# Latent attention's scores by row halves with stacked rotary parts, and each attention step's scores placed behind the values of the step before it

## The chip, the cores and the metric

The kernel runs on one core of one Trainium2 chip. The metric is the device time of one execution in microseconds (us); three runs of the kernel before gave 1801.73, 1802.9 and 1808.01 us, median 1802.9. The engines are TensorE (PE; its weight loads are a row of their own, PEld), VectorE (DVE), ScalarE (ACT), GpSimd (POOL) and SyncE (SP, which issues most DMAs).

## The reference

A two-layer backbone works on 512 latent tokens and 256 context tokens of width 1024. In each layer one input projection feeds four groups, whose outputs are concatenated and projected back; a squared-ReLU MLP follows. The groups are neighbourhood attention (A), banded window attention (B), latent attention (C) and a state-space scan (D). The change is mostly in C, cut here to what matters:

```
q  = (rmsnorm(cq)  @ w_uq ).reshape(B, L, 4, 64 + 32)    # 4 heads, 64 plain + 32 rotary features
kv = (rmsnorm(ckv) @ w_ukv).reshape(B, L, 4, 64 + 64)
qn, qr = q[..., :64], q[..., 64:];  kn, v = kv[..., :64], kv[..., 64:]
qr, kr = axial_rope(qr), axial_rope(kr)                  # latent tokens; kr is one for all heads
s = (einsum('bqhd,bkhd->bhqk', qn, kn) + einsum('bqhd,bkd->bhqk', qr, kr)) * 96 ** -0.5
p = softmax(s);  o = einsum('bhqk,bkhd->bqhd', p, v)
```

A latent query sees all 768 keys, a context query only the 256 of the context. In the second layer the context's outputs are not needed, so there are no context queries.

## The kernel before

Products are made in fp32r from split operands: x = hi + lo, and hi·hi, lo·hi and hi·lo are added up in PSUM. `dense` (L247 on, its matmuls on L261) makes 24 matmuls of 128 rows for each block of 128 outputs and each segment (512 latent or 256 context tokens). A weight block comes by DMA from SP, ACT casts the high part (L238) and DVE makes the low one (L239).

All three attentions go through `attend` (L390). One call is a *step*: 128 queries, two heads. It makes the scores in banks of the PSUM pool `ps_s` (4 banks of 512 columns, also used by the preparation of latent attention and by the scan), the row minimum on DVE (L441 with two key parts, L449 with one), the exponential on ACT (L455), reciprocal and scaling (L460, L462 on DVE with two parts, L464 on ACT with one), the transposes of the probabilities on TensorE (L473), their copies to SBUF (L374 ACT, L376 DVE) and the product with the values (L479). The last value matmul of each step is appended to the list `anchors`. Window and neighbourhood attention call it with `paired=True`: heads lie in rows 0 to 63 and 64 to 127, and their score matmuls alternate (L418), each placed behind the one before it. Latent attention's heads have 96 rows, its scores are made head by head (L431), and no score is tied to another step.

A step has 768 score columns per head in latent attention when its queries are latent (a *full* step; 4 banks for two heads), and 256 when they are context tokens (a *context* step). The first layer has 12 latent steps (two head pairs with 4 full steps and 2 context steps each), the second 8 full ones. They are called A1, A2 and so on here, and those of window attention B1, B2 and so on.

Instructions are put in order ahead of time by a list scheduler: on each engine the earliest instruction of the program that is ready by its simulated clock comes next. `tc.issue_after(x)` forbids an instruction to come before x on its engine. Other work is interleaved in program order by `merge(*(generator, weight))`, which always advances the generator with the smallest (count + 0.5) / weight. Beside latent attention (weight 12 in the first layer, 11 in the second) runs `calls` (weight 6 and 11): in the first layer the projections sq1 and sk, three rotary steps, and the projections nq0, nk0, nq1, nk1; in the second the same without sq1. Each goes through `behind` (LAG = 2), so that it comes after the values of the last step but one of those already in the program. Beside window attention's 12 and 8 steps run six convolution projections and two for gates (weights 11 and 12), beside neighbourhood attention's the scan and the first half of the output projection.

Before its steps the latent generator (`mla`) normalises, makes the queries (`queries`, L1031), rotates their rotary part, copies both parts into one 96-row tile per head (L1035, L1038, L1048), transposes the rotary key (L1056) and writes it into each head's key tile as hi and lo (L1020, L1021), and makes the plain keys (L1063) and values (L1069). The yields in it count for `merge`: queries, rotary keys, plain keys, values, then the steps.

The norm ahead of the MLP ends in `rest`, a generator: its first advance makes the sums and the reciprocal root on DVE, the second the broadcast on TensorE (L308), the others the modulated activations of the last token piece. The first NAHEAD blocks of the MLP (3 and 5) advance it.

Of the kernel before, what the change touches and what calls it, by code (L numbers as in the profile page):

```python
# [72 lines left out]
QORD = (0, 1, 2)  # L73
# [18 lines left out]
def kernel(ctx: ExitStack, tc: tile.TileContext, D: dict, out: bass.AP, dbg=None):  # L92
# [157 lines left out]
    def dense(src, acts, segs, evac, ks=range(KD), w=None, low=V, midway=None):  # L250
# [139 lines left out]
    def attend(q, k, parts, sinks, vt, put, sgn=-1.0, paired=False):  # L390
# [14 lines left out]
        if paired:  # L405


            off, prev = 0, None
            for k0, n, tab in parts:
                if off == 0 or off + n - b0 > 512:  # L410
                    banks, b0 = (pss(), pss()), off
                dst = [banks[a][:, off - b0:off - b0 + n] for a in range(2)]
                nmm = len(terms(0))
                for i in range(nmm):
                    for a in range(2):
                        x, y = terms(a)[i]
                        with (tc.issue_after(prev.ins) if prev else nullcontext()):
                            prev = PE.matmul(dst[a], x, y[:, k0:k0 + n], start=i == 0, stop=i == nmm - 1)  # L418
                for a in range(2):
                    ats[a].append((dst[a], off, n, tab))  # L420
                off += n
        else:
            for a in range(2):
                off = 0
                for k0, n, tab in parts:
                    if off == 0 or off + n - b0 > 512:
                        bank, b0 = pss(), off
                    dst = bank[:, off - b0:off - b0 + n]
                    mm = terms(a)
                    for i, (x, y) in enumerate(mm):  # L430
                        PE.matmul(dst, x, y[:, k0:k0 + n], start=i == 0, stop=i == len(mm) - 1)  # L431
                    ats[a].append((dst, off, n, tab))
                    off += n
# [205 lines left out]
    for l in range(DEPTH):  # L639
# [329 lines left out]
        def mla():  # L969
# [36 lines left out]
            for b in range(4):  # L1006
# [4 lines left out]
            qh = [unit("u", nm("qh")) for _ in range(4)]  # L1011
            kh = [(unit("u", nm("kh"), F32R), unit("u", nm("kl"), F32R)) if SR[2] else unit("u", nm("kh"))
                  for _ in range(4)]

            def put_k(hd, r0, r1, c0, n, ps):
                if not SR[2]:
                    evac(kh[hd][r0:r1, c0:c0 + n], ps)
                    return
                hi, lo = (x[r0:r1, c0:c0 + n] for x in kh[hd])
                A.copy(hi, ps)  # L1020
                V.tensor_tensor(lo, ps, hi.bitcast(F32), ALU.subtract)  # L1021

            vm = [unit("u", nm("vm")) for _ in range(2)]

            def queries():
                msc = -(96.0 ** -0.5)
                for b in QORD:
                    for s, c0, n in segs:
# [4 lines left out]
                        if b < 2:  # L1033
                            for e in range(2):
                                A.activation(qh[2 * b + e][0:64, c0:c0 + n], ps[64 * e:64 * e + 64, :n], AF.Copy, scale=msc)  # L1035
                        elif s == 1:
                            for hd in range(4):
                                A.activation(qh[hd][64:96, c0:c0 + n], ps[32 * hd:32 * hd + 32, :n], AF.Copy, scale=msc)  # L1038
                        else:
                            qr, qs = unit("q", nm("qr")), unit("q", nm("qs"))  # L1040
                            A.activation(qr[:, :SEQ], ps, AF.Copy, scale=msc)
# [4 lines left out]
                            for hd in range(4):  # L1046
                                rs_ = slice(32 * hd, 32 * hd + 32)
                                V.tensor_tensor(qh[hd][64:96, 0:SEQ], qr[rs_, :SEQ], qs[rs_, :SEQ], ALU.add)  # L1048
# [4 lines left out]
            for s, c0, n in full:  # L1053
                pk = pss()
                for t in range(n // P):
                    PE.transpose(pk[0:32, t * P:(t + 1) * P], krr[:, c0 // P + t, :], ident)  # L1056
                for hd in range(4):
                    put_k(hd, 64, 96, c0, n, pk[0:32, 0:n])
            yield
            for b in range(2):  # L1060
                for s, c0, n in full:
                    ps = pss()
                    PE.matmul(ps[:, :n], wkv[:, b * P:(b + 1) * P], ckv[:, c0:c0 + n], start=True, stop=True)  # L1063
                    for e in range(2):
                        put_k(2 * b + e, 0, 64, c0, n, ps[64 * e:64 * e + 64, :n])
# [8 lines left out]
            for b in range(2):  # L1074
                om = unit("u", nm("om"))
                for j in range(WS // P):
# [7 lines left out]
                    qs = [qh[2 * b + a][0:96, cs] for a in range(2)]  # L1084
                    ks = [kh[2 * b + a] for a in range(2)]
                    if SR[2]:
                        qs = [tuple(x[0:96] for x in split_q(x, 96)) for x in qs]
# [381 lines left out]
```

## Time and profile before

| | |
|---|---|
| Profiled execution, its own time | 1802.71 us |
| its span, first to last instruction | 1800.9 us |
| PE busy | 1750.6 us (97%) |
| DVE busy | 1109.4 us (62%) |
| ACT busy | 737.8 us (41%) |
| POOL busy | 240.3 us (13%) |
| mean granted clock of TensorE | 0.987 |
| chain that ended last, PE's share | 89% |

Busy times are unions of an engine's instruction spans. Matmuls overlap in a pipeline, so the time that one costs is the distance from its start to the next one's start, not its own duration. The granted clock is 1.00 at 2.4 GHz and 0.50 at 1.2 GHz.

### The profile page before, as it was taken

How to read it: one execution, taken by the hardware profiler on the slowest of the kernel's cores; microseconds unless marked ns; L12 is line 12 of the kernel's file. 1: busy time of each engine (PE TensorE's matmuls, PEld its weight loads, DVE VectorE, ACT ScalarE, POOL GpSimd, SP SyncE). 2: the span in 40 equal slices, each digit the busy share in tenths (PEclk: the TensorE clock that was granted, in tenths of full speed). 3: DMA queues.
4: the chain of work that ended last, by engine and by line, in shares of the span. 5: the costliest groups of instructions: out<-in, count | busy, mean ns of one | idle time of the engine just before them, and what ended most of it. 6: DMA issues, size and time to landing. Idle time of an engine off the chain costs nothing.

```text
span 1800.9 us, 28892 instructions
## 1 busy us (share of the span) xinstructions
PE 1750.6 (97%) x11170; PEld 1493.3 (83%) x11170; DVE 1109.4 (62%) x2372; ACT 737.8 (41%) x1497; POOL 240.3 (13%) x367
## 2 busy tenths in 40 slices
PE   8999999999989999999999999999989999999998
PEld 7877877777878888888888998688878898888888
DVE  5548458688677566467555674757779563444355
ACT  4347546655353123123123443545544451323244
POOL 0102011234320000000000331101114310000002
PEclk8999999999999999999999999899999999999999
DMA  9440267632635445344444534111333543222333
GB/s 337 138 152 17 67 214 248 214 115 93 211 109 177 136 153 163 109 154 144 155 135 146 173 113 138 35 36 36 120 110 104 199 146 100 94 94 94 106 104 119
DMA packets 86249, 238.94 MB, mean 133 GB/s; under 512 B 9200, under 2 KB 17392, under 8 KB 86112
## 3 DMA queue, kind: packets, MB, share of 16 engines
q1 hardware_dynamic: 74976, 208.57, 35.8%
q0 software_dynamic: 7104, 24.33, 3.8%
q10 hardware_dynamic: 4032, 4.20, 0.7%
q8 instruction: 88, 1.44, 0.3%
q14 instruction: 49, 0.40, 0.1%
HBM read 214.52 MB, written 22.54 MB: 132 GB/s over the span
## 4 chain that ended last, share of the span: by engine, by line
PE 89%; DVE 6%; DMA 2%; ACT 1%; issue 1%; POOL 0%; DVEq 0%; ACTq 0%; POOLq 0%; SPq 0%
PE pt L261 68%; PE pt L479 3%; PE pt L473 3%; PE pS L666 2%; PE pS L431 2%; PE pS L418 2%; PE pt L172 1%; PE pt L666 1%; PE pt L296 1%; PE pt L933 1%; PE pS L1031 1%; DVE pr L441 1%; DVE wl L239 1%; PE pt L864 0%; DMA old<-in_hT_dram 0%
## 5 line engine op out<-in xcount | busy, mean ns | idle before, releaser
L238 ACT CAST wh<-wr 128x1024 fp32r<-128x1024 f32 x206 | 215.9, 1049 | 403.0 <-PE pt L261 291.2
L239 DVE TENSOR_TENSOR wl<-wr,wh 128x1024 fp32r<-128x1024 f32 x206 | 253.9, 1233 | 100.5 <-ACT wh L238 96.0
L261 PE MATMUL pt<-ah,wh 128*128 128x512 f32 (+1 forms) x1304 | 275.0, 352 | 7.1 <-ACT ah L346 3.1
L261 PE MATMUL pt<-al,wh 128*128 128x512 f32 (+1 forms) x1304 | 269.5, 347 | 0.0
L261 PE MATMUL pt<-ah,wl 128*128 128x512 f32 (+1 forms) x1304 | 268.7, 348 | 0.0
L261 PEld LDWEIGHTS pt<-ah,wh 128*128 128x128 f32 x1304 | 213.3, 190 | 48.0 <-ACT ah L346 4.3
L261 PEld LDWEIGHTS pt<-ah,wl 128*128 128x128 f32 x1304 | 215.2, 191 | 31.4 <-issue 0.8
L261 PEld LDWEIGHTS pt<-al,wh 128*128 128x128 f32 x1304 | 212.9, 190 | 31.1 <-issue 2.4
L261 PE MATMUL pt<-hh,wh 128*128 128x256 f32 (+1 forms) x896 | 168.2, 330 | 0.0
L261 PE MATMUL pt<-hl,wh 128*128 128x256 f32 (+1 forms) x896 | 167.0, 329 | 0.0
L261 PE MATMUL pt<-hh,wl 128*128 128x256 f32 (+1 forms) x896 | 166.9, 329 | 0.0
L1291 DVE SCALAR_TENSOR_TENSOR h<-pt,mod,h 128x512 f32<-128x512 f32 (+1 forms) x112 | 66.3, 595 | 153.8 <-PE pt L261 153.6
L261 PEld LDWEIGHTS pt<-hh,wh 128*128 128x128 f32 x896 | 137.6, 189 | 17.7 <-issue 0.6
L261 PEld LDWEIGHTS pt<-hh,wl 128*128 128x128 f32 x896 | 138.0, 190 | 15.4
L261 PEld LDWEIGHTS pt<-hl,wh 128*128 128x128 f32 x896 | 138.1, 190 | 15.0
L208 DVE SCALAR_TENSOR_TENSOR ma<-wm,cact,ma 128x768 f32<-128x768 f32 x112 | 109.9, 1013 | 65.3 <-DMA wm<-in_w_mod_dram 65.2
L1281 ACT ACTIVATE r<-pt 128x512 f32<-128x512 f32 (+1 forms) x101 | 51.4, 509 | 237.1 <-PE pt L261 237.1
L1283 DVE TENSOR_TENSOR r<-r 128x512 f32<-128x512 f32 (+1 forms) x101 | 58.2, 577 | 123.0 <-ACT r L1281 122.9
L322 POOL TENSOR_TENSOR sq<-sq,sq 128x256 f32<-128x256 f32 x66 | 64.7, 980 | 442.9 <-ACT sq L318 442.2
L455 ACT ACTIVATE pr<-pr,m 128x512 f32<-128x512 f32 (+2 forms) x96 | 77.8, 811 | 40.3 <-DVE m L441 38.4
L261 PE MATMUL pt<-oh,wo 128*128 128x256 f32 (+1 forms) x576 | 93.9, 306 | 0.0
L261 PEld LDWEIGHTS pt<-oh,wo 128*128 128x128 f32 x576 | 79.0, 194 | 5.5 <-issue 1.7
(295 smaller groups left out, 2473.5 us busy)
## 6 DMA issues: line engine op xcount, KB each, us to landing
wr<-in_w_mlp_dram SPq DMA_DIRECT2D x154, 512.0 KB, 3.5
wo<-oscr SPq DMA_DIRECT2D x66, 512.0 KB, 4.7
wm<-in_w_mod_dram SPq DMA_DIRECT2D x80, 384.0 KB, 3.6
wr<-in_w_a_dram SPq DMA_DIRECT2D x36, 512.0 KB, 4.1
wm<-in_w_mod_dram SPq DMA_DIRECT2D x32, 512.0 KB, 4.0
wr<-in_w_out_dram SPq DMA_DIRECT2D x16, 512.0 KB, 4.3
oscr<-wh POOLq DMA_DIRECT2D x16, 512.0 KB, 3.7
oscr<-wl POOLq DMA_DIRECT2D x16, 512.0 KB, 5.6
```

Of the source, the lines that this page charges most:

```text
L208: V.scalar_tensor_tensor(a[:, :T], w, cact[:, k, i:i + 1], a[:, :T], ALU.mult, ALU.add)
L238: A.copy(wh, raw)
L239: low.tensor_tensor(wl, raw, wh.bitcast(F32), ALU.subtract)
L261: PE.matmul(ps[:, :n], w[:, k - k0, :], acts[k][a][:, c0:c0 + n], start=i == 0, stop=i == len(mm) - 1)
L322: G.tensor_tensor(sq[0][:, :n], sq[0][:, :n], q[:, :n], ALU.add)
L455: A.activation(pr[:, :off], src, AF.Exp, scale=-1.0 if tabs else sgn, bias=mcol, accum_out=s2[:, a:a + 1])
L473: PE.transpose(pt[:, i * P:(i + 1) * P], probs[a][:, (g0 + i) * P:(g0 + i + 1) * P], ident)
L479: last_mm = PE.matmul(pv[64 * a:64 * a + 64, :P], vt(a, t), pts[a][:, t * P:(t + 1) * P], start=t == 0, stop=t == nkt - 1)
L666: PE.matmul(acc[t], acts[k][a][:, t * P:(t + 1) * P], slabs[pc][w][:, kk, :], start=k == 0 and x == 0, stop=k == KD - 1 and x == 2)
L1281: A.activation(r[:, :n], ps, AF.Relu)
L1283: V.tensor_tensor(r2[:, :n], r[:, :n], r[:, :n], ALU.mult)
L1291: V.scalar_tensor_tensor(h[d][:, c0:c0 + n], ps, mod[:, 40 + d, s:s + 1], h[d][:, c0:c0 + n], ALU.mult, ALU.add)
```

## The change

Latent attention's plain parts (64 rows each) of two heads lie in one tile, as window attention's do. Its rotary parts are stacked: in rows 64a to 64a + 31 of `qst` lies head a's rotary query as hi, in the next 32 rows as lo; `kst` holds the rotary key four times below one another, one tile with hi and one with lo. A step's scores have five products per head and key part, all by row halves: three plain ones and two stacked ones. The queries are copied whole (128 rows), the rotary ones come first (`QORD`), are split once, and go to `qst` by eight DMAs from POOL's queue per layer. The keys are split once for two heads, the rotary key once for all. The yield behind the rotary keys is gone, and a step calls `split_q` once, not twice.

In `attend` the branch for unpaired heads is gone, and the first score of a step is placed behind `anchors[-1]`, the last value matmul of the step before it, in all three attentions. The advances of `rest` move: the second comes after 6 (first layer) or 18 (second layer) matmuls of the second MLP block, not right behind the first block.

```diff
-QORD = (0, 1, 2)
+QORD = (2, 0, 1)
+RQ = 0
...
-                if midway and i == len(mm) // 2:
-                    midway()
+                if midway and i == midway[0]:
+                    midway[1]()
...
-            return [(q[a][0], k[a][0]), (q[a][1], k[a][0]), (q[a][0], k[a][1])]
+            return [(q[a][0], k[a][0]), (q[a][1], k[a][0]), (q[a][0], k[a][1]), *extra[a]]
...
-            off, prev = 0, None
+        off, prev = 0, anchors[-1] if anchors else None
+        for k0, n, tab in parts:
+            if off == 0 or off + n - b0 > 512:
+                banks, b0 = (pss(), pss()), off
+            dst = [banks[a][:, off - b0:off - b0 + n] for a in range(2)]
+            nmm = len(terms(0))
+            for i in range(nmm):
                 for a in range(2):
+                    x, y = terms(a)[i]
+                    with (tc.issue_after(prev) if prev else nullcontext()):
+                        prev = PE.matmul(dst[a], x, y[:, k0:k0 + n], start=i == 0, stop=i == nmm - 1).ins
...
+            k4 = unit("q", nm("k4"))
+            A.copy(k4[:, :T].rearrange("p (t r e) -> p t r e", r=4, e=32),
+                   krr[:, :, None, :].to_broadcast([P, 6, 4, 32]))
+            for s, c0, n in full:
+                pk = pss()
+                for t in range(n // P):
+                    PE.transpose(pk[:, t * P:(t + 1) * P], k4[:, c0 + t * P:c0 + (t + 1) * P], ident)
+                hi, lo = (x[:, c0:c0 + n] for x in kst)
+                A.copy(hi, pk[:, 0:n])
+                V.tensor_tensor(lo, pk[:, 0:n], hi.bitcast(F32), ALU.subtract)
...
+                        dst = qn[b] if b < 2 else qr
+                        A.activation(dst[:, c0:c0 + n], ps[:, :n], AF.Copy, scale=msc)
...
+                    if b == 2:
+                        hi, lo = unit("q", nm("qrh"), F32R), unit("q", nm("qrl"), F32R)
+                        A.copy(hi[:, :WS], qr[:, :WS])
+                        V.tensor_tensor(lo[:, :WS], qr[:, :WS], hi[:, :WS].bitcast(F32), ALU.subtract)
+                        for hd in range(4):
+                            for i, x in enumerate((hi, lo)):
+                                r0 = 64 * (hd % 2) + 32 * i
+                                (G, nc.scalar)[RQ].dma_start(qst[hd // 2][r0:r0 + 32, :WS].bitcast(F32),
+                                                             x[32 * hd:32 * hd + 32, :WS].bitcast(F32))
...
-            for s, c0, n in full:
-                pk = pss()
-                for t in range(n // P):
-                    PE.transpose(pk[0:32, t * P:(t + 1) * P], krr[:, c0 // P + t, :], ident)
-                for hd in range(4):
-                    put_k(hd, 64, 96, c0, n, pk[0:32, 0:n])
-            yield
...
-                    for e in range(2):
-                        put_k(2 * b + e, 0, 64, c0, n, ps[64 * e:64 * e + 64, :n])
+                    hi, lo = (x[:, c0:c0 + n] for x in kn[b])
+                    A.copy(hi, ps[:, :n])
+                    V.tensor_tensor(lo, ps[:, :n], hi.bitcast(F32), ALU.subtract)
...
+                    x = split_q(qn[b][:, cs], P)
+                    attend([rows(x, a, slice(0, P)) for a in range(2)], [rows(kn[b], a) for a in range(2)],
+                           part, None, vt, lambda ps, om=om, cs=cs: evac(om[:, cs], ps),
+                           extra=[[(rows(qst[b], a, cs), rows(y, a)) for y in kst] for a in range(2)])
...
-                    ahead.append(up_block(qd, f, parts[:1], midway=None if f else lambda: next(rest)))
-                    for _ in range(PACE[l] - (f == 0)):
+                    now = (12, (6, 18)[last], None)[min(f, 2)]
+                    ahead.append(up_block(qd, f, parts[:1], midway=now and (now, lambda: next(rest))))
+                    for _ in range(PACE[l] if f else 0):
                         next(rest, None)
```

## Rows read from the trace of the kernel before

**Rows 1.** The page's first part: busy time, share of the span, instructions.
```profile
PE 1750.6 (97%) x11170; PEld 1493.3 (83%) x11170; DVE 1109.4 (62%) x2372; ACT 737.8 (41%) x1497; POOL 240.3 (13%) x367
```

**Rows 2.** Busy by stretch: window, its length, PE, PEld, DVE, ACT, POOL, clock, DMA.
```profile
100.00:142.50 42.50, 42.28 (x210) 29.26 (x209) 20.61 (x38) 20.51 (x42) 1.29 (x2) 1.00 0.38 124
142.50:177.20 34.70, 34.46 (x279) 27.84 (x278) 30.27 (x96) 26.48 (x71) 10.31 (x18) 1.00 0.06 17
177.20:237.20 60.00, 60.00 (x435) 47.52 (x433) 28.03 (x76) 28.18 (x66) 4.15 (x12) 1.00 0.27 87
...
1120.00:1153.50 33.50, 30.64 (x118) 19.85 (x117) 20.34 (x33) 16.25 (x32) 2.51 (x7) 0.95 0.21 63
```

**Rows 3.** Timeline of PE, latent scores: start, us, engine, line, tiles, form, count.
```profile
143.81 0.39 PE L431 MATMUL pS<-kh,nqh 96*128 96x512 f32 x1
...
144.87 0.40 PE L431 MATMUL pS<-kh,nqh 96*128 96x512 f32 x1
```

**Rows 4.** The same view where window attention's scores begin: pairs, between transposes.
```profile
210.45 0.38 PE L418 MATMUL pS<-oh,nqh 64*128 64x256 f32 x1
210.76 0.44 PE L473 MATMUL pt<-con,pr 128*128 128x128 f32 x2
211.13 0.38 PE L418 MATMUL pS<-oh,nqh 64*128 64x256 f32 x1
...
211.59 0.39 PE L418 MATMUL pS<-oh,nql 64*128 64x256 f32 x2
211.71 0.39 PE L418 MATMUL pS<-ol,nqh 64*128 64x256 f32 x2
```

**Rows 5.** Groups by form, 142.5 to 177.2: a step's softmax, and copies.
```profile
L455 ACT ACTIVATE pr<-pr,m 128x768 f32<-128x768 f32 x11 | 10.3, 937 | 0.9 <-DVE m L441 0.9
...
L441 DVE CUSTOM_DVE_ANT_0 pr<-pS,zero,mx 128x512 f32<-128x512 f32 x11 | 8.2, 746 | 0.2
...
L462 DVE TENSOR_SCALAR pr<-pr,s 128x768 f32<-128x768 f32 x10 | 6.4, 640 | 0.1
...
L441 DVE CUSTOM_DVE_ANT_0 pr<-pS,zero 128x256 f32<-128x256 f32 x12 | 5.0, 418 | 0.8 <-PE pS L431 0.6 <-PE pt L473 0.2
...
L374 ACT COPY pT<-pt 128x512 f32<-128x512 f32 x8 | 4.6, 579 | 0.3 <-PE pt L473 0.3
```

**Rows 6.** Timeline of PE: transposes, a rotary step, and a step's values.
```profile
149.87 0.82 PE L473 MATMUL pt<-con,pr 128*128 128x128 f32 x6
150.53 1.02 PE L1105 MATMUL pt<-sq,con 128*128 128x512 f32 x2
150.99 0.80 PE L431 MATMUL pS<-kh,nqh 96*128 96x512 f32 x1
...
152.62 1.53 PE L479 MATMUL pt<-pT,vm 128*64 128x128 f32 x24
154.09 0.39 PE L431 MATMUL pS<-kh,nqh 96*128 96x256 f32 x1
```

**Rows 7.** Busy times of stretches with little on PE, and of those behind them.
```profile
514.10:517.50 3.40, 0.82 (x5) 0.74 (x6) 3.18 (x9) 1.72 (x3) 0.00 (x0) 1.00 0.00 0
517.55:520.90 3.35, 3.35 (x10) 2.56 (x9) 2.50 (x6) 2.42 (x6) 1.48 (x2) 0.50 0.48 155
...
1155.80:1159.20 3.40, 1.79 (x8) 1.13 (x9) 3.40 (x10) 0.90 (x2) 0.87 (x2) 1.00 0.00 0
1159.25:1166.00 6.75, 6.75 (x24) 5.75 (x24) 6.71 (x22) 5.06 (x12) 1.68 (x3) 0.50 0.01 2
```

**Rows 8.** Groups by form, 104 to 142.5: low parts of the keys, first layer.
```profile
L1021 DVE TENSOR_TENSOR kl<-pS,kh 64x512 fp32r<-64x512 f32 x4 | 2.8, 688 | 2.9 <-ACT kh L1020 2.9
```

**Rows 9.** Groups of POOL: what the issue of one DMA takes there.
```profile
L508 POOL DMA_DIRECT2D oscr<-wh x16 | 8.9, 554 | 473.1 <-ACT wh L238 449.6 <-ACT raw L374 9.4 <-ACT pT L374 8.3
```

**Rows 10.** Timeline of PE: waits at the norm and for the scan's copies.
```profile
516.68 0.43 PE L308 MATMUL pt<-con,rs 128*128 128x128 f32 x2 [3.01 <-DVE rs L288]
...
1321.20 0.38 PE L418 MATMUL pS<-nk,nqh 64*128 64x256 f32 x1 [2.15 <-DVE xw L853]
```

More of the change, by code (lines that the diff above doesn't have):

```diff
@@ L387, in behind, with attend @@
             fn()
-    def attend(q, k, parts, sinks, vt, put, sgn=-1.0, paired=False):
+    def attend(q, k, parts, sinks, vt, put, sgn=-1.0, extra=((), ())):
         tabs = len(parts) > 1
@@ L401, in terms @@
                 return [(q[a], k[a])]
-            return [(q[a][0], k[a][0]), (q[a][1], k[a][0]), (q[a][0], k[a][1])]
+            return [(q[a][0], k[a][0]), (q[a][1], k[a][0]), (q[a][0], k[a][1]), *extra[a]]
         ats = ([], [])
-        if paired:
-            off, prev = 0, None
[L409 to L418, printed above, removed]
+        off, prev = 0, anchors[-1] if anchors else None
[5 more added lines that the diff above has]
+            for i in range(nmm):
                 for a in range(2):
-                    ats[a].append((dst[a], off, n, tab))
-                off += n
-        else:
+                    x, y = terms(a)[i]
+                    with (tc.issue_after(prev) if prev else nullcontext()):
+                        prev = PE.matmul(dst[a], x, y[:, k0:k0 + n], start=i == 0, stop=i == nmm - 1).ins
             for a in range(2):
[L424 to L433, printed above, removed]
+                ats[a].append((dst[a], off, n, tab))
+            off += n
         for a in range(2):
@@ L1010, in mla @@
             V.tensor_copy(krr[:, 4:6], kr[:, 4:6])
[L1011 to L1021, printed above, removed]
-            vm = [unit("u", nm("vm")) for _ in range(2)]
+            qn = [unit("u", nm("qn")) for _ in range(2)]
+            kn = [(unit("u", nm("kh"), F32R), unit("u", nm("kl"), F32R)) for _ in range(2)]
+            qst = [unit("u", nm("qst"), F32R) for _ in range(2)]
+            kst = [unit("u", nm("kst"), F32R) for _ in range(2)]
+            vm = [unit("u", nm("vm")) for _ in range(2)]
+            k4 = unit("q", nm("k4"))
[8 more added lines that the diff above has]
+                V.tensor_tensor(lo, pk[:, 0:n], hi.bitcast(F32), ALU.subtract)
             def queries():
                 msc = -(96.0 ** -0.5)
+                qr, qs = unit("q", nm("qr")), unit("q", nm("qs"))
                 for b in QORD:
@@ L1082, in vt @@
                         return vm[t // 3][:, (t % 3) * 256 + hd * 64:(t % 3) * 256 + hd * 64 + 64]
[L1084 to L1087, printed above, removed]
-                        ks = [tuple(x[0:96] for x in y) for y in ks]
-                    else:
-                        ks = [x[0:96] for x in ks]
-                    attend(qs, ks,
-                           part, None, vt, lambda ps, om=om, cs=cs: evac(om[:, cs], ps))
+                    x = split_q(qn[b][:, cs], P)
+                    attend([rows(x, a, slice(0, P)) for a in range(2)], [rows(kn[b], a) for a in range(2)],
+                           part, None, vt, lambda ps, om=om, cs=cs: evac(om[:, cs], ps),
+                           extra=[[(rows(qst[b], a, cs), rows(y, a)) for y in kst] for a in range(2)])
                     yield
@@ L1138, in swa @@
                            [nsink[:, hd:hd + 1] for hd in (b, b + 2)], vt,
-                           lambda ps, os_=os_, cs=cs: evac(os_[:, cs], ps), paired=True)
+                           lambda ps, os_=os_, cs=cs: evac(os_[:, cs], ps))
                     yield
@@ L1198, in put @@
                             evac(on[:, cs], ps)
-                    attend([rows(x, a, slice(0, P)) for a in range(2)], [rows(blocks["nk", b], a) for a in range(2)], part, None, vt, put, sgn=1.0, paired=True)
+                    attend([rows(x, a, slice(0, P)) for a in range(2)], [rows(blocks["nk", b], a) for a in range(2)], part, None, vt, put, sgn=1.0)
                     if j == 3:
```

14 lines of the change are left out of this document (2 added, 12 removed).

## The prediction

> **What bounds the kernel now.** I read the page first: TensorE is busy for 97% of the span, no other engine for more than 62% [rows 1]. So only two things can move the end: TensorE's work itself, and idle time put into it or taken from it. Then the busy times by stretch, for the attention stages. In the first layer TensorE works 42.28 of 42.50 us while the queries and keys are prepared, and 34.46 of 34.70 and 60.00 of 60.00 in the latent steps, at granted clock 1.00; VectorE is the runner-up with 30.27 of 34.70 [rows 2]. In the second layer's preparation it is idle for 2.9 us, and the clock is 0.95 (last of [rows 2]). The reader is to see that there is next to no hole to fill in the first layer, although one step's softmax is a long chain. The reason is lookahead: scores of the next one or two steps run under the softmax of this one. From 142.5 to 177.2 the six steps A1 to A6 pass with only three short rotary steps as other work, because the merge puts nq0 behind the seventh step. It is this lookahead that the change forbids.
>
> **The change part by part.**
>
> *Scores by row halves.* One head's 768 columns now take 144.87 - 143.81 = 1.06 us for three products [rows 3], 0.35 per product, a pair of heads 2.12. By row halves two heads' matmuls start together and the next pair follows 0.12 us later for 256 columns (211.59 and 211.71 in [rows 4]), as one 96-row matmul does. Five paired products cost 5 x 0.35 = 1.75 us: 0.37 less for a full step, 0.12 less for a context step. 16 full and 4 context steps: -6.4 us. Bounds: -6.4 if the halves overlap as they do there, and +14 if they did not overlap at all (ten products instead of six); I take the first, since the row is the same shape of work. Against it stands the Trainium skill, "TensorE: Matmul & The Clock Gate", section "LDWEIGHTS (loading the stationary operand)": a load costs by its columns, whatever its rows, 107 ns for 128. By that rule alone, as an estimate, a step's 20 loads take 2.1 us, the gain is zero, and the sum below ends 6 us higher. The trace disagrees for loads into different halves: two loads with their two matmuls pass in 0.12 us [rows 4].
>
> *Switching between row halves and whole rows.* A lone score start to the transposes behind it is 0.31 us where 0.12 is its own, and two transposes of 0.11 to the next score take 0.37 [rows 4]: 0.1 to 0.2 us for each crossing. Latent steps get one crossing more (scores to transposes): 20 x 0.1 = +2. The 40 window and neighbourhood steps lose fragments of scores between transposes: at one or two crossings each -4 to -8. I take -4, net -2.
>
> *The wait for the values of the step before.* Behind a waiting score stands everything later on TensorE's queue: its own transposes and values, and all scores of later steps. What remains is the chain of one full step [rows 5, 6]: minimum of head a 0.42 + 0.75 + two reads of 0.08 (some 1.25 with the hops), of head b the same, exponential of b 0.94 with 0.2 for its sum and hop, reciprocal 0.15, scaling 0.64, b's last transposes 0.6, copy 0.58, values 1.46 (152.62 to 154.09), and some 0.4 for the remaining hops: 7.3 us from the last score to the last value. TensorE works 2.9 of them (12 transposes at 0.11, 24 value matmuls). So a full step without other work leaves 4.4 us idle; a context step, with half the minimum and a third of the keys, about 2.7.
>
> Which steps lack other work? First layer: counting yields with weights 12 and 6, and one yield less, the program order is queries, sq1, keys, values, sk, A1, A2, rotary, A3, A4, rotary, A5, A6, rotary, A7, A8, nq0, A9, A10, nk0, A11, A12, nq1, nk1. A1 has sk; A8, A10 and A12 have a projection of 24 x 0.23 + 24 x 0.12 = 8 us. A2, A3, A4, A7, A9 (5 x 4.4) and A5, A6, A11 (3 x 2.7) have none but three rotary steps of some 0.87 each (from 150.53, and the score behind it ends at 151.79, 0.4 later than its own length lets expect [rows 6]): 30.1 - 2.6 = +27.5. Second layer: sk, nq0, nk0, nq1, nk1 and the first convolution cover A1 to A5 and A8; A6 and A7 are bare: +8.8. In window attention the eight projections are used up by B8 (first layer, four steps left) and B5 (second, three left). What is left there is the scan's opening, which no edge holds: bounds 0 and 2 x 13.5, I take +4, nearer to cover. In neighbourhood attention scan and output projection stand beside each step: 0, bounds -9 (the waits for the scan's copies such as the 2.15 us at 1321.20 [rows 10] vanish) and +16 (half of a 4 us hole in eight steps).
>
> *The clock.* After 3.4 us with 0.82 of work on TensorE the next 3.35 ran at 0.50, after 3.4 with 1.79 the next 6.75 [rows 7]. The bare steps work 4.9 of 9.3 us in lumps. Ten 512-column matmuls took 3.35 us at 0.50 where 0.23 each is 2.3: one such stretch costs 1.1 us or more. Bounds: 0, and two stretches in each of ten bare steps, +22. I take one in half of them, +6.
>
> *Preparation.* Low parts of the keys cost DVE 0.69 each per head and part [rows 8]; with whole rows a quarter of the rotary ones and half of the plain ones remain, likewise ACT's copies. In the first layer TensorE is full there and nothing is gained. In the second it stood idle 2.9 us and ran some 3.4 us at half clock (0.95 over 33.5 us, last of [rows 2]): -5, bounds 0 and -8. The eight DMAs of `qst` take POOL 8 x 0.55 = 4.4 us [rows 9], some 18 us ahead of A1's first stacked score with sq1 between: nothing; without that cover their landing, bounded by the issue time and twice that, 4 to 9 us once per layer.
>
> *The norm.* The broadcast waited 3.01 us on TensorE [rows 10]; six matmuls of 0.23 now come ahead of it: -1.4. In the second layer no such wait stands there: 0.
>
> Sum: -6.4 - 2 + 27.5 + 8.8 + 4 + 6 - 5 - 1.4 = +31.5 us. On the profiled execution's own 1802.7 us (0.2 below the median of the runs shown) that is 1834 us.
>
> **The rivals.**
>
> *Faster, 1788 us.* Scores ahead of time hold two to four of `ps_s`'s four banks, which the preparation and the scan share, and they break up the transposes. If the holes are covered, because sq1 and sk, 16 us together, come to lie under A1 to A3 once the preparation is quicker, and the scan's opening under the last window steps, there remain -6.4 (scores), -6 (switches), -5 (second layer's preparation), -1.4, and the waits for the scan's copies, -9, with some 13 us of holes left against before: about -15. For it: VectorE's and the banks' waits exist. Against it: sq1 and sk come earlier in the program than every step and are taken first, and A2 to A7 stay bare. It decides from the point where a bare step idles under 1 us on average.
>
> *No change, 1803 us.* The holes cost 16 us net and the savings give them back, if A2 to A4 are half covered. For it speaks only that the order is fixed by a simulated clock whose times I don't know; same reasons against.
>
> *Much slower, 1874 us.* The chain lengthens because VectorE, 87% busy in A1 to A6 [rows 2], works in order, and the bare steps run mostly at half clock: a 1.5 us longer chain in the 32 full steps of window and neighbourhood attention is +48 where no cover is left, half of it +24, and the clock's upper bound adds 16: +71 in all. For it: the clock's fall behind sparse stretches [rows 7]. Against: without lookahead VectorE has less to do at once.
>
> **How the numbers follow.** Forecast 1834 (its own range 1812 to 1856) 0.48; much slower 0.12; no change 0.12; faster 0.28. A difference of 0.5%, 9 us, is about what a measurement of this kernel can tell from none. So faster 0.28, same 0.12, slower 0.60. For 8 in 10 the range leaves out the far half of the faster case and of the much slower one: 1784 to 1862.
>
> **What would show it.** Right: in 142 to 190 us the latent steps come as scores, hole, transposes, values, with TensorE's busy share near 0.6 and idle time ended by the scaled probabilities of L462; the clock at 0.50 in several stretches there; values of A6 end some 10 us later than now, A12's 20 or more. Pairs of scores 0.12 us apart at 256 columns in latent attention, one crossing per step. The wait at the norm's broadcast is 1.4 us shorter. Wrong: TensorE as full as now between 142 and 237 us, or projections lying between A2 and A7.

## The result, and the profile after

The changed kernel takes 2113.57 us (median of four runs, 2108.64 to 2118.32), the kernel before beside it 1803.65: ratio 1.171, 95% interval 1.168 to 1.175. The forecast was 1834, with a range from 1784 to 1862. The side was right; the loss is 310 us where 31 were forecast, ten times as much.

The page's first part and its clock slices, after (to be read against [rows 1]):

```profile
PE 1839.8 (87%) x11314; PEld 1561.4 (74%) x11314; DVE 1103.2 (52%) x2348; ACT 732.1 (35%) x1452; POOL 234.1 (11%) x363
...
PEclk9997897878899999999999999877778899999999
```

TensorE is busy for 89 us *more* than before, and the span grew by 308, so it is idle for 219 us more. VectorE, ScalarE and POOL have a little less to do. No engine became the bound: an idle hole, and a slow clock behind it.

Where the time lies, from the two traces (us; TensorE's busy time in brackets). Latent attention's stretch begins with its first score; each attention's stretch ends with its last value matmul, and the next begins there.

| stretch | before | after | difference |
|---|---|---|---|
| up to the first latent score | 142.6 | 141.9 | -0.7 |
| latent attention, layer 1 | 88.2 (88.0) | 138.7 (96.1) | +50.5 |
| window attention, layer 1 | 123.3 (119.0) | 215.5 (151.2) | +92.2 |
| neighbourhood attention, layer 1 | 101.9 (96.6) | 127.4 (105.9) | +25.5 |
| to the MLP's first down matmul | 125.3 (116.7) | 127.4 (117.4) | +2.1 |
| MLP, and layer 2's preparation | 572.3 | 566.0 | -6.3 |
| latent attention, layer 2 | 83.2 (81.5) | 126.4 (91.5) | +43.2 |
| window attention, layer 2 | 82.3 (82.3) | 147.1 (101.5) | +64.8 |
| neighbourhood attention, layer 2 | 80.1 (71.7) | 115.6 (85.2) | +35.5 |
| the rest | 401.8 | 403.1 | +1.3 |

Six attention stages hold 311.7 us of loss, the other stretches give 3.6 back. The view of [rows 2] for the changed kernel, with its columns: first the stretches that answer to three of its rows (both preparations, and 142.5 to 177.2), then three attention stages whole.

```profile
100.00:141.90 41.90, 41.90 (x211) 29.39 (x210) 12.25 (x23) 12.23 (x26) 4.83 (x10) 1.00 0.39 119
142.50:177.20 34.70, 18.70 (x154) 15.53 (x152) 16.04 (x45) 12.32 (x26) 3.25 (x5) 0.78 0.15 46
...
1283.30:1316.80 33.50, 33.31 (x151) 24.55 (x149) 14.06 (x29) 10.77 (x21) 5.86 (x12) 1.00 0.33 95
```
```profile
141.90:280.60 138.70, 96.05 (x681) 75.74 (x679) 55.79 (x152) 47.58 (x111) 7.47 (x17) 0.80 0.11 35
280.60:496.10 215.50, 151.20 (x915) 118.77 (x914) 93.50 (x221) 81.21 (x184) 21.53 (x52) 0.82 0.41 136
...
1443.20:1590.30 147.10, 101.48 (x587) 82.17 (x585) 66.95 (x167) 49.36 (x109) 9.33 (x29) 0.79 0.18 59
```

In 142.5 to 177.2 TensorE's share fell from 0.99 to 0.54, at a mean clock of 0.78. The preparations went the other way: VectorE's 20.61 us became 12.25 in the first layer, and in the second TensorE has no hole left.

A bare latent step on TensorE (start, us, line, tiles, form, count, idle before it and its releaser):

```profile
167.34 0.50 PE L418 MATMUL pS<-kh,nqh 64*128 64x512 f32 x2
...
168.15 0.63 PE L418 MATMUL pS<-kst,qst 64*128 64x512 f32 x4
168.61 0.28 PE L418 MATMUL pS<-kh,nqh 64*128 64x256 f32 x2
...
168.97 0.40 PE L418 MATMUL pS<-kst,qst 64*128 64x256 f32 x4
172.91 2.79 PE L461 MATMUL pt<-con,pr 128*128 128x128 f32 x12 [3.54 <-DVE pr L450]
176.28 2.77 PE L467 MATMUL pt<-pT,vm 128*64 128x128 f32 x24 [0.58 <-ACT pT L375]
178.98 0.50 PE L418 MATMUL pS<-kh,nqh 64*128 64x512 f32 x2
```

The order is the one forecast: scores, hole, transposes, values, and the idle time, 4.12 us, is close to the 4.4 forecast. But the transposes take 2.79 us where 12 at 0.11 were expected (six took 0.82 in [rows 6]), and the values 2.77, not 1.53 [rows 6]. The next rows (windows again, with the mean granted clock after POOL's entry: a hole and what lies behind it, in a latent and in a window step) answer to [rows 7] and show why.

```profile
158.40:162.00 3.60, 0.11 (x2) 0.00 (x0) 2.91 (x10) 2.22 (x5) 0.45 (x1) 0.97 0.00 0
162.00:164.80 2.80, 2.74 (x13) 2.77 (x14) 1.21 (x3) 0.87 (x2) 0.00 (x0) 0.50 0.00 0
...
382.90:388.90 6.00, 0.00 (x0) 0.00 (x0) 6.00 (x13) 4.62 (x12) 1.55 (x3) 0.85 0.64 207
388.90:395.40 6.50, 6.49 (x21) 5.22 (x22) 3.09 (x5) 1.47 (x3) 0.16 (x3) 0.62 0.38 132
```

Behind the latent hole the granted clock is 0.50, the level of 1.2 GHz; in the 6.5 us behind the window hole its mean is 0.62. The last two rows lie in window attention, in steps that have a whole projection each. This is the same place as TensorE's instructions:

```profile
382.20 0.38 PE L418 MATMUL pS<-oh,nqh 64*128 64x256 f32 x2
...
388.92 1.11 PE L461 MATMUL pt<-con,pr 128*128 128x128 f32 x4 [6.10 <-ACT pr L452]
389.68 3.76 PE L262 MATMUL pt<-ah,wh 128*128 128x512 f32 x8
393.24 2.31 PE L262 MATMUL pt<-ah,wl 128*128 128x512 f32 x8
395.39 1.29 PE L262 MATMUL pt<-al,wh 128*128 128x512 f32 x5
396.61 0.66 PE L467 MATMUL pt<-pT,vs 128*64 128x128 f32 x8
...
399.90 1.12 PE L262 MATMUL pt<-al,wh 128*128 128x256 f32 x8
400.95 0.40 PE L418 MATMUL pS<-oh,nqh 64*128 64x256 f32 x2
```

The cover is there and does not cover: the projection stands between a step's transposes and its values, and behind the values. Then the scores come, and behind the scores there is nothing for 6.10 us. The next step's scores come at 400.95, so this step, one of context queries, takes 18.75 us. The waits of TensorE for the probabilities in window attention of the first layer (line, waited for: us, times, longest) say the same:

```profile
PE pt L461 <- DVE s L448: 29.4, 4, 11.2
PE pt L461 <- ACT pr L452: 17.8, 4, 6.2
PE pt L461 <- ACT e L446: 8.5, 2, 4.2
```

The holes of the steps that have a projection are not all of one size: in B2 to B9 they are 4.2 to 11.2 us and add up to 50, where the bare steps behind them show 3.4 at most. The longest ends at 325.79:

```profile
317.96 0.09 DVE L429 DVE_READ_ACCUMULATOR2_ANT m<- 128x1 f32 x1
...
320.16 1.04 ACT L239 CAST wh<-wr 128x1024 fp32r<-128x1024 f32 x1 [4.00 <-DMA wr<-in_w_a_dram]
321.11 0.82 ACT L443 ACTIVATE pr<-pr,m 128x640 f32<-128x640 f32 x1
...
325.79 2.37 PE L461 MATMUL pt<-con,pr 128*128 128x128 f32 x10 [11.18 <-DVE s L448]
```

The first head's row minimum is there at 318.05. Its exponential starts at 321.11, because ScalarE has the cast of a weight block ahead of it, and that cast had waited 4.00 us for its DMA. So other work does not only fail to cover the hole, it also makes it longer.

### The profile page after: what moved, and what is told of

The parts are those of the page before. It is cut to its first block, busy times and chain, and to the rows that moved or that the text cites. A ratio compares the mean times of both kernels' runs of the same rounds, so it can differ in the third digit from the quotient of the medians.

```text
span 2109.0 us, 29167 instructions
## 1 busy us (share of the span) xinstructions
PE 1839.8 (87%) x11314; PEld 1561.4 (74%) x11314; DVE 1103.2 (52%) x2348; ACT 732.1 (35%) x1452; POOL 234.1 (11%) x363
## 4 chain that ended last, share of the span: by engine, by line
PE 78%; DVE 13%; ACT 4%; DMA 3%; issue 2%; POOL 0%; SPq 0%; DVEq 0%; ACTq 0%; POOLq 0%
PE pt L262 60%; PE pt L461 5%; PE pt L467 4%; DVE pr L429 3%; PE pS L418 2%; PE pS L654 2%; ACT pr L443 2%; DVE acc L793 2%; DVE pr L450 1%; DVE wl L240 1%; PE pt L654 1%; PE pt L297 1%; PE pt L921 1%; PE pS L1023 1%; DMA wr<-in_w_out_dram 1%
## 5 line engine op out<-in xcount | busy, mean ns | idle before, releaser
L262 PE MATMUL pt<-ah,wh 128*128 128x512 f32 (+1 forms) x1304 | 298.0, 373 | 9.8 <-ACT ah L344 5.3
L461 PE MATMUL pt<-con,pr 128*128 128x128 f32 x512 | 112.5, 385 | 215.1 <-DVE pr L450 119.7
L262 PEld LDWEIGHTS pt<-ah,wh 128*128 128x128 f32 x1304 | 230.5, 204 | 56.1 <-ACT ah L344 6.3
L461 PEld LDWEIGHTS pt<-con,pr 128*128 128x128 f32 x512 | 85.5, 197 | 238.1 <-issue 137.2
L1273 DVE SCALAR_TENSOR_TENSOR h<-pt,mod,h 128x512 f32<-128x512 f32 (+1 forms) x112 | 66.3, 596 | 151.4 <-PE pt L262 151.2
```

What stands on the lines that cost most here:

```text
L461: PE.transpose(pt[:, i * P:(i + 1) * P], probs[a][:, (g0 + i) * P:(g0 + i + 1) * P], ident)
L1273: V.scalar_tensor_tensor(h[d][:, c0:c0 + n], ps, mod[:, 40 + d, s:s + 1], h[d][:, c0:c0 + n], ALU.mult, ALU.add)
```

## The experiments

Eleven kernels ran. The theory after the result: the wait alone makes the loss, through holes (steps without other work, and steps whose other work is out of phase) and through the clock behind them. Rivals: the stacked scores are dear; VectorE and ScalarE, in order, lengthen the chain.

**e1_no_wait**: the changed kernel without the wait.

```diff
-        off, prev = 0, anchors[-1] if anchors else None
+        off, prev = 0, None
```

> The changed kernel without the wait: a step's first score is placed behind nothing, all else as changed. Theory (the wait for the values of the step before makes the whole loss, by the holes it leaves and the half clock behind them): 1788 us (1775 to 1800), which is the forecast's other terms alone: -6.4 scores, -2 to -4 crossings, -5 preparation of the second layer, -1.4 norm. Rival 1 (stacking, row halves, the eight DMAs or the new order of the queries cost a good part of it in the latent stage): over 1850 us.

Measured 1819.05 us, ratio 1.0077 (1.006 to 1.0094). The wait is 294 of the 310 us. But the time is 19 us over the range that was expected: the rest of the change, which was to gain some 15 us, costs 14.

**e2_before_wait**: the kernel before, with the wait alone, in both branches of `attend`.

```diff
             off, prev = 0, None
+            head = anchors[-1] if anchors else None
...
-                        with (tc.issue_after(prev.ins) if prev else nullcontext()):
+                        with (tc.issue_after(prev.ins if prev else head) if prev or head else nullcontext()):
...
-                        PE.matmul(dst, x, y[:, k0:k0 + n], start=i == 0, stop=i == len(mm) - 1)
+                        with (tc.issue_after(anchors[-1]) if anchors else nullcontext()):
+                            PE.matmul(dst, x, y[:, k0:k0 + n], start=i == 0, stop=i == len(mm) - 1)
```

> The kernel before with the wait alone: each step's scores behind the last value matmul of the step before, in all three attentions, everything else as before. Theory: 2100 to 2150 us, as slow as the changed kernel or a little slower, since it lacks the shorter scores. Rival 1: under 1950 us.

Measured 2095.81, ratio 1.161 (1.159 to 1.164), with window attention at 206.0 and 146.9 us. The wait alone makes the loss, on either kind of scores. It was expected to be as slow as the changed kernel or slower, for want of the shorter scores; it is 18 us faster, and 14 of them lie in latent attention (134.0 and 116.9 us against 138.7 and 126.4). The first rows show a bare latent step of this kernel, TensorE and VectorE's first minimum; the row below them is the first minimum of the changed kernel's step that starts at 167.34:

```profile
177.02 0.50 PE L433 MATMUL pS<-kh,nqh 96*128 96x512 f32 x1
...
178.18 0.39 PE L433 MATMUL pS<-kh,nqh 96*128 96x512 f32 x1
178.38 0.42 DVE L443 CUSTOM_DVE_ANT_0 pr<-pS,zero 128x256 f32<-128x256 f32 x1 [0.50 <-PE pS L433]
...
181.71 2.61 PE L475 MATMUL pt<-con,pr 128*128 128x128 f32 x12 [2.31 <-DVE pr L464]
```
```profile
169.40 0.42 DVE L429 CUSTOM_DVE_ANT_0 pr<-pS,zero 128x256 f32<-128x256 f32 x1 [1.19 <-PE pS L418]
```

Head by head, the first head's minimum starts 1.36 us after the step's first score, while the second head's scores (from 178.18) still run. In pairs both heads are ready only when the whole pass is over, 2.06 us after the first score. The transposes follow 4.69 us after the first score here and 5.57 us in the changed kernel, and the step takes 10.64 us against 11.64 (177.02 to 187.66, and 167.34 to 178.98). So where scores wait, pairing them makes a step longer, although TensorE passes them faster.

**e3_latent_only**: the changed kernel with the wait in latent attention alone.

```diff
-        off, prev = 0, anchors[-1] if anchors else None
+        off, prev = 0, anchors[-1] if anchors and extra[0] else None
```

> The changed kernel with the wait in latent attention alone; window and neighbourhood steps may run ahead. Theory (each stage pays for its own wait; between the traces the two latent stages grew by 50 and 43 us): 1788 + 94, so 1865 to 1900 us, with window stages about as long as before (123 and 82 us). Rival 2 (the late latent stage upsets what follows, by weights that come late and work that bunches, and window attention's own wait matters little): over 1980 us, window stages still near 215 and 147 us.

Measured 1902.17, ratio 1.054 (1.052 to 1.056). The time is 2 us over the expected range. Latent attention takes 136.9 and 124.5 us, window attention 133.0 and 83.0: each stage pays for its own wait, and the window stages are within 3 us of e1_no_wait's. The latent wait, which held 36.3 of the 40.3 us of forecast idle time, makes 83 us over e1_no_wait; the other two attentions' make 211.

**e4_one_ahead**: the first score is placed behind the values of the last step but one.

```diff
-        off, prev = 0, anchors[-1] if anchors else None
+        off, prev = 0, anchors[-2] if len(anchors) > 1 else None
```

> The changed kernel with the wait one step looser: a step's first score behind the values of the last step but one, so that scores may run one step ahead. Theory: the next step's scores, transposes and values cover most of the hole, a step then has two chains in flight: 1785 to 1830 us. Rival 3 (any fixed order between steps' scores and values makes TensorE's queue wait for VectorE, one step of lookahead is not enough): over 1880 us.

Measured 1857.26, ratio 1.029 (1.026 to 1.032). That is over the expected range and under the rival's 1880. One step of lookahead gives back 256 of the 310 us, though not all. Latent attention is at 98.4 and 92.5 us, window attention of the first layer at 150.7, against 94.4, 85.8 and 135.4 with no wait: 26 of the 38 us that are left over e1_no_wait lie in these three stages.

**e5_in_phase**: the wait stays; the other work is put into the program behind the scores of the next step, and on TensorE not ahead of them.

```diff
+        while pending:
+            with tc.issue_after(prev):
+                pending.pop(0)()
         for a in range(2):
             pr = unit("pr", nm("pr"))
...
-                behind(f)
+                pending.append(f)
                 yield
+            while pending:
+                behind(pending.pop(0))
```

> The kernel after, with one edit: each interleaved piece of other work (projections, rotary steps, pieces of the output projection) is put into the program right behind the scores of the next step and on TensorE not ahead of them, where before it was put behind the step. In the kernel after the window steps come on TensorE as transposes, first part of a projection, values, rest of the projection, scores, hole of 6 us: the cover is there, but out of phase. Theory (phase): with scores, projection, transposes, values the holes of the steps that have a projection close: window attention 215.5 us to about 145 in the first layer, 147.1 to about 100 in the second, neighbourhood attention about 10 shorter in each; total about 1975 us (1930 to 2020). Rival (VectorE and ScalarE in order, and the weight transfer, lengthen the softmax chain whenever a projection runs): the hole stays or moves ahead of the projection; window attention of the first layer stays over 190, total over 2060.

Measured 1959.36, ratio 1.086 (1.083 to 1.090): 154 us less than after, as the phase theory has it in sum. Window attention takes 164.7 and 110.4 us, more than expected, neighbourhood attention 109.1 and 87.5, less; the second layer's latent attention falls from 126.4 to 111.8 us, while the first layer's ends only 1.3 us earlier (279.3). TensorE in a window step of context queries:

```profile
349.07 0.38 PE L419 MATMUL pS<-oh,nqh 64*128 64x256 f32 x2
...
349.62 2.12 PE L262 MATMUL pt<-ah,wh 128*128 128x512 f32 x8
...
358.17 1.06 PE L173 MATMUL pt<-wm,cact 128*32 128x512 f32 x8
359.17 0.66 PE L465 MATMUL pt<-con,pr 128*128 128x128 f32 x4
362.87 1.12 PE L471 MATMUL pt<-pT,vs 128*64 128x128 f32 x8 [3.04 <-ACT pT L375]
363.92 0.58 PE L419 MATMUL pS<-oh,nqh 64*128 64x256 f32 x2
```

Scores, projection, transposes, values: 14.85 us instead of 18.75. Ahead of the transposes there is no hole left; the projection of the changed kernel ran at the wrong time. The rival has a part in what remains. The values wait 3.04 us for a copy on ScalarE, which has a weight block's cast (itself held 1.58 us by its DMA) and the convolution's work ahead of it. Such waits make 10.2 us in this stage (line, waited for: us, times, longest):

```profile
PE pt L471 <- ACT pT L375: 10.2, 10, 3.0
PE pt L465 <- DVE pr L454: 8.8, 4, 3.4
PE pt L465 <- ACT pr L456: 5.5, 2, 3.4
```

Of the 14.3 us of waits for the probabilities, 9.2 belong to the last steps, which have no projection left; the forecast had +4 for such steps, in both layers together. A bare step's hole is 3.4 us there; the 6.10 of a step with a projection, after, was longer, so work that ScalarE and VectorE do in order did lengthen the chain as well. Of the 140 us that are left over e1_no_wait, 40 lie before the end of the first layer's latent attention (279.3 against 239.0 us), 26 in the second's, 29 in each window stage.

**e6_filled_holes**: 12 matmuls of 512 columns (6 in context steps) behind each latent step's scores, into a bank that nothing reads.

```diff
...
+        if extra[0]:
+            idle = pst()
+            for i in range(12 if off > 512 else 6):
+                with tc.issue_after(prev):
+                    prev = PE.matmul(idle, kst[0][:, 0:P], kst[0][:, 0:512], start=True, stop=True).ins
...
```

> The kernel after, with 12 matmuls of 512 columns (6 in context steps) added behind the scores of each latent step, into a bank that nothing reads: work for TensorE in the hole, 2.8 us of 3.5. They do nothing for the result. Theory (the clock falls behind the hole and the transposes and values after it pay for that): a step's 12 transposes pass in about 1.3 us instead of 2.8 and the values in 1.5, so the latent stage of the first layer takes about 120 us instead of 138.7, that of the second about 112 instead of 126.4; total about 2080 us (2060 to 2098), although more work is done. Rival (the hole itself is the loss, the clock adds little): total 2110 to 2150, both stages as long as they were or longer by what does not fit the hole.

Measured 2089.98, ratio 1.159 (1.155 to 1.162): more work, 24 us less time. The latent stages take 124.1 and 112.5 us, 28.5 less than after. TensorE in a latent step:

```profile
167.25 0.50 PE L418 MATMUL pS<-kh,nqh 64*128 64x512 f32 x2
...
169.20 3.01 PE L426 MATMUL pt<-kst 128*128 128x512 f32 x12
172.72 1.86 PE L466 MATMUL pt<-con,pr 128*128 128x128 f32 x12 [0.51 <-DVE pr L455]
175.36 1.53 PE L472 MATMUL pt<-pT,vm 128*64 128x128 f32 x24 [0.79 <-ACT pT L375]
176.82 0.50 PE L418 MATMUL pS<-kh,nqh 64*128 64x512 f32 x2
```

The step takes 9.57 us instead of 11.64 (167.34 to 178.98 after). Transposes and values together are 2.17 us shorter, which is what the clock alone had cost in such a step.

**e7_yield_back**: e1_no_wait with an empty yield behind the queries.

```diff
                 yield from queries()
+            yield
             for b in range(2):
```

> The kernel after without the wait (the first score of a step behind nothing) as in e1_no_wait, which took 1819.05 us, and with the yield that the change took out of latent attention's preparation put back, so that the projections stand at their old places in the program. Theory (the missing yield put sq1 and sk ahead of A1, so that nothing lay under A1 and A2, where TensorE stood idle 3.6 us): about 1808 us (1800 to 1813), latent and window attention of the first layer together 217 us or less instead of 229.8. Rival (the stacked scores themselves are dearer where they mix with other work: both heads' banks are taken at once, and each crossing between row halves and whole rows costs 0.1 us or more): 1815 to 1825.

Measured 1812.83, ratio 1.0046 (1.003 to 1.0062): 6 us of the 14. Latent and window attention of the first layer together take 216.3 us instead of 229.8, as the theory has it, and the total lies at the upper end of its range. In e1_no_wait the scores of A2 had waited for the minima of A1 with nothing beside them:

```profile
152.43 1.25 PE L418 MATMUL pS<-kh,nqh 64*128 64x256 f32 x2 [3.58 <-DVE m L429]
```

**e8_old_norm**: e7_yield_back with the norm's advances where they were before.

```diff
-                if midway and i == midway[0]:
-                    midway[1]()
+                if midway and i == len(mm) // 2:
+                    midway()
...
-                    now = (12, (6, 18)[last], None)[min(f, 2)]
-                    ahead.append(up_block(qd, f, parts[:1], midway=now and (now, lambda: next(rest))))
-                    for _ in range(PACE[l] if f else 0):
+                    ahead.append(up_block(qd, f, parts[:1], midway=None if f else lambda: next(rest)))
+                    for _ in range(PACE[l] - (f == 0)):
```

> The kernel e7_yield_back (no wait, old yields; 1812.83 us) with the advances of the second norm put back where they were in the kernel before. Theory (the later broadcast takes its own wait of 3.0 us away, but the activations of the context tokens come later too, and four matmuls of the next block wait 4.6 us for them): the stretch from the last value of neighbourhood attention to the first down matmul of the MLP goes from 129.0 back to about 125.3 us, total about 1809 us (1805 to 1812). Rival (that stretch is longer for another reason): no difference, 1811 to 1815.

Measured 1808.45, ratio 1.0015 (1.0005 to 1.0025): another 4.4 us, as the theory has it. TensorE in the changed kernel, to be read against [rows 10]:

```profile
684.27 0.38 PE L309 MATMUL pt<-con,rs 128*128 128x128 f32 x2
...
691.79 0.62 PE L262 MATMUL pt<-ah,wh 128*128 128x256 f32 x3 [0.97 <-ACT wh L239]
693.81 1.92 PE L262 MATMUL pt<-ah,wh 128*128 128x256 f32 x9 [1.40 <-ACT ah L344]
697.70 1.01 PE L262 MATMUL pt<-ah,wh 128*128 128x256 f32 x3 [1.98 <-ACT ah L344]
699.45 0.58 PE L262 MATMUL pt<-ah,wh 128*128 128x256 f32 x1 [0.74 <-ACT ah L347]
```

The broadcast no longer waits 3.01 us, but the block behind it now meets activations that are late, 4.1 us in three waits, and a weight's high part that is late, 0.97 us. The mean clock of the whole stretch is 0.93 in e7_yield_back and 0.99 in this kernel.

**e9_pipelined**: e8_old_norm with a latent step's transposes and values behind the scores of the next step.

```diff
+        while tails:
+            with tc.issue_after(prev):
+                tails.pop(0)()
...
+        if extra[0]:
+            tails.append(tail)
+        else:
+            tail()
```

> The kernel e8_old_norm with a latent step's transposes and values put into the program behind the scores of the next step, and on TensorE not ahead of them, so that the scores run one step ahead by construction. Theory (without the wait the stacked scores lose their gain to being broken up by transposes, 0.1 to 0.2 us a crossing): latent attention of the first layer from 93.7 to about 88 us, of the second from 87.2 to about 84; total 1798 to 1805 us, level with or a little under the kernel before. Rival (VectorE's chain and the banks set the pace of those steps, not the order on TensorE): within 3 us of e8_old_norm, 1806 to 1812.

Measured 1810.24, ratio 1.0032 (1.0022 to 1.0042). The total is the rival's, within 2 us of e8_old_norm, but not for the rival's reason, for the order did act: preparation and latent attention of the second layer took 5.4 us less, latent attention of the first 9.5 more.

**e10_min_forward**: e8_old_norm with the minimum's order of reading turned round in latent attention.

```diff
-                for i, (ps, o0, n, tab) in enumerate(reversed(at)):
+                for i, (ps, o0, n, tab) in enumerate(at if extra[0] else reversed(at)):
```

> The kernel e8_old_norm (no wait, old yields, old norm; 1808.45 us, 0.15% over the kernel before) with one edit: in latent attention the row minimum reads the banks of the first key part first, not last. These two banks are the ones that the next step's first pair of scores waits for. Theory (since the heads' scores are now made in pairs, a step needs the banks of both heads at once, and the minimum of the second head frees its first bank last: waits of 1.5 us in the first layer and 3.9 us in the second): about 1805 us (1802 to 1808). Rival (the banks come free early enough in nearly all steps): within 2 us of e8_old_norm, 1806 to 1811.

Measured 1805.86, ratio 1.0013 (1.0002 to 1.0024). The time falls into the theory's range, but the ratios of e8_old_norm and of this kernel overlap: no effect shown.

**e11_pipelined_2**: e9_pipelined's order in the second layer alone.

```diff
-        if extra[0]:
+        if extra[0] and later:
             tails.append(tail)
```

> The kernel e8_old_norm with the one step's pipelining of e9_pipelined in the second layer alone. In e9_pipelined the second layer's preparation and latent attention, from the first layer's last matmul on, took 5.4 us less than in e8_old_norm and window attention 1.8 less, while the first layer took 10 us more. Theory (the two layers are independent): 1808.45 - 7 = about 1801.5 us (1798 to 1804), level with the kernel before or 0.1% under it. Rival (the gain there came from work that the first layer's order had moved): 1805 to 1811.

Measured 1803.19, ratio 0.9985 (0.9972 to 0.9999). The changed kernel without its wait, with the old yield, the old norm and this order is level with the kernel before, as the theory had it: 0.15% under it, with an interval that ends 0.01% under it.

## Why the prediction was wrong

The mechanism was right in kind: the wait forbids lookahead, the bare latent steps come as forecast, and their idle time ends with the scaled probabilities. It was wrong in which steps it strikes. Step by step:

- **Which steps lack other work** is the step that failed. A step counted as covered if a projection stood beside it in program order, and so window attention was put at +4 and neighbourhood attention at 0. They lost 157 and 61 us. TensorE's queue had the projection between transposes and values and behind them, outside the hole. A hole is covered only by what comes *between the scores and the transposes* on the queue. e5_in_phase shows it: the same work in that place gives 154 us back, nearly all of it in window and neighbourhood attention and in the second layer's latent attention. The scan's opening covered the last window steps no better. The latent stages suffered too: A1, counted as covered by sk, idles 7.81 us ahead of its transposes, and A6's values end 23.5 us later (200.70 against 177.25), where some 10 was forecast; TensorE idles 42.65 and 34.8 us there (length less busy time) against 0.2 and 1.7, where +27.5 and +8.8 were forecast. Why the list scheduler puts the projection there (its simulated times) was not looked into.
- **The clock** was put at +6, bounds 0 to 22, by counting a half-speed stretch in half of ten bare steps. TensorE's busy time rose by 89 us for nearly the same work. In the latent stages alone e6_filled_holes gets 28.5 us back. The trace has 51 stretches at 0.50 against 9 before; by the mean clock (0.919 of 2109 us, 0.987 of 1801) they hold 342 us against 47. Of the 51, 46 lie in the six attention stages, which have 60 steps, against 2 before: most steps paid, not five, and the term grew with the first mistake. Its unit was too small as well. Of the ten matmuls of [rows 7] two had started ahead of the stretch; eight started in it, 0.43 us apart where 0.23 is usual, so that stretch cost some 1.6 us, not 1.1, and a bare latent step lost 2.17 (e6_filled_holes). The Trainium skill, "TensorE: Matmul & The Clock Gate", section "HAM oscillation — how this bites in real kernels", tells of a kernel in which every short burst behind a wait pays for the clock's fall again; the trace agrees, with 0.50 in 162.0 to 164.8.
- **The chain** of a full step was right: 4.4 us idle forecast, 4.12 measured; for a context step 2.7 against 2.57 (1.96 and 0.61 in the step whose scores start at 190.19).
- **Scores**: in a clean step a full score pass takes 1.63 us to the start of its last four matmuls, and those pass in 0.24: 1.87 us, against 1.75 forecast and 2.12 before. So the gain on TensorE is two thirds of the one forecast. The Trainium skill's rule on loads ("TensorE: Matmul & The Clock Gate", "LDWEIGHTS (loading the stationary operand)"), 107 ns for each of 20 loads one after the other, would make it 2.1, as an estimate: the trace disagrees. But in a kernel whose scores wait, the term has the wrong sign: the pairs bring the first minimum later, and a bare step takes 1.0 us more, not 0.37 less (e2_before_wait). Nor did the gain show without the wait: the scores of a step were broken up by transposes, and in e7_yield_back, whose first latent stage ran at clock 1.00, TensorE's time from start to start (idle times left out) adds up to 23.1 us for that stage's scores against 22.5 before, and to 0.139 us for a transpose against 0.119. Why the scores in pairs fit worse between the transposes was not separated from the banks' waits, and the -2 for crossings was not measured apart. The bound of +14 for halves that do not overlap is mis-added as well: ten products of 0.35 us instead of six are 1.4 us more in each of 16 full steps, +24 with the context steps; the sum did not use it.
- **Preparation**: the second layer's took 85.7 us instead of 91.8 from the MLP's last matmul to the first score, -6.1 against -5. Right.
- **The norm**: -1.4 forecast, +2.1 in the changed kernel, and 4.4 measured by putting it back. The wait that goes was named, the activations that are late next were not.
- **The yield** that went was costed at nothing; without the wait it costs 6 us.
- **The rivals**: "much slower" (1874) named window and neighbourhood attention, but with the chain grown by 1.5 us as the cause; that is a part, and by more than 1.5 us a step: at 3.4 us each the holes of B2 to B9 would be 27 us instead of 50. Phase and clock are the larger parts. "Faster" fails even without the wait (e1_no_wait).

## What to carry to other kernels

When an edge forbids an engine to look ahead, follow the queue, not the program: list what stands between the instruction that starts the chain and the one that waits for its end. Work on either side of that gap covers nothing, however much there is. And a hole that recurs was paid twice on TensorE here, once as idle time and once at half clock behind it; price the second from the number of holes, all of them. Price an instruction order by when the first result is ready for the waiting engine, too: pairs of scores passed faster and still made a waiting step longer.

## What was not expected of the hardware

Matmuls that nothing reads made the kernel faster: 2.8 us of them in a hole of 3.5 shortened a step from 11.64 to 9.57 us. Two matmuls in different row halves pass in 0.23 us at 512 columns and 0.12 at 256, as one does alone, also where their operands are stacked parts.
